# Branch C's values taken next to A's, a one-tile rotary table, lambdas first, and a last product in whole blocks and halves

## The chip, the cores and the metric

The kernel runs on one core of a Trainium2 chip. Its time is device microseconds (us) of one execution. The engines are TensorE (PE in the profile; PEld are its weight loads), VectorE (DVE), ScalarE (ACT), GpSimd (POOL) and SyncE (SP), which only issues transfers. Each works through its own queue in order and waits there for semaphores.

## What is computed

Two layers over 512 tokens of width 1024, and a last RMSNorm. Cut to what matters:

```
h = rmsnorm(x, norm_g)
aq, ak, av, az, buv, bz, cq, ck, cv, cz, gl = split_cols(h @ w_in)
A: qa, ka = partial_rope(aq), partial_rope(ak)
   ya = rmsnorm(diff_attention(qa, ka, av, lam)) * silu(az)
B: yb = u * (causal chunk product of layernorm(gelu(v))) * silu(bz)
C: yc = (three dilated windows with v = cv, merged) * silu(cz)
merged = sum over n of sigmoid(gl_n) * (y_n @ w_branch[n])
x = x + merged @ w_out
```

`partial_rope` turns the first 16 of 64 channels by sine and cosine of position times frequency. `lam` is one number a layer, from four short vectors.

## The kernel before

Everything is kept transposed: channels on the 128 partitions, the 512 tokens along the free axis. All products run in pairs of high and low parts (`xh`, `xl` for x, `whi`, `wlo` for weights): three matmuls for each product, high by high, low by high, high by low.

**Weights.** They come as tiles `raw` of 128x1024 (512 KB) over SP's queue, two tiles deep. `slot` (L151) turns each half into a slot: ACT copies the high part to `whi` (L159), and the low part `wlo` is a subtraction (L160), every fifth on GpSimd and the others on VectorE. There are six `whi` and five `wlo` buffers, so slots are made some five ahead of TensorE. Slots of the last layer's product `w_out` from block 3 on are written straight into `xh` and `xl`, and two into `mh` and `ml`, which are free by then.

**Order of the work.** `plan()` (L49) lists the dense items of a layer. First come `vb` (B's v), `val` of A, `split` and `mix` and the first pair of A. `vb` and `val` A use `proj_M` (L446): x is the stationary operand, 512 weight columns stream, and four token blocks are summed in four banks; x is the unnormalised `xuh`/`xul` there, and the norm's factor is applied when the bank is emptied. `split` makes `xh`/`xl` of the normalised x, which all later items read, and `mix` makes `mh`/`ml`. Then the two attentions run (`attention_a`, `attention_c`); between their steps `fill()` (L1029) pulls dense items, as many as `cost()` allots to the stretch. `val` of C stands at the end of A's list; it uses `proj_N` (L435) with 256 streamed columns and the normalised x. After C follow the gates and branch products, and `out`.

**The last product.** `i_out` (L789) multiplies by `w_out` in eight blocks of 128 channels. In the last layer it does so for the left 256 tokens in all eight blocks and then for the right 256, whose first block is followed by the final norm of the left half (`final(LT)`); `final(RT)` ends the kernel.

**The rotary table.** `tables()` (L301) splits position times frequency into two parts, multiplies each by five pieces of 1/(2 pi) and reduces each product to a fraction of a turn, in steps of 128x32 on GpSimd. ACT takes sine and cosine, and `trig` goes through DRAM (L352) into `cosr` and `sinr`, on the same SP queue as the weights. `lambdas()` (L358) loads `tab` and `lam_in` and computes lambda on VectorE and ACT; it is called in the first layer's `split`.

A scheduler sets each engine's order from the code, a priority for the slots and its own estimate of times.

Of the kernel before, what the change touches and what calls it, by code (L numbers as in the profile page):

```python
# [34 lines left out]
LOMOD = 5  # L35
FILLS = 25
# [12 lines left out]
def plan():  # L49

    start = [("vb",), ("val", BR_A), ("split",), ("mix",), ("pp", BR_A, 0)]
    a = [("pp", BR_A, 1), ("pp", BR_A, 2), ("u2", 0)] + [("pp", BR_A, i) for i in range(3, 6)] + [("vbn",), ("u2", 2), ("pp", BR_C, 0), ("val", BR_C)]
# [16 lines left out]
def item_units(it):  # L69
    kind = it[0]  # L70
    if kind == "vb" or it == ("val", BR_A):
        return [("M", C_VB if kind == "vb" else C_AV, k) for k in range(4)]
    if kind == "val":
        return [("N", C_CV + 256 * b, k) for b in range(2) for k in range(2)]
# [25 lines left out]
def hybrid_kernel(ctx: ExitStack, tc, xT, posr, wpack, tabs, cvec, pvec, rvec, lamv, sguw, outT):  # L100
# [62 lines left out]
    def weights():
        for l in range(DEPTH):
            for g in GROUPS:
# [67 lines left out]
    cv = const.tile([P, 8], F32, name="cv")  # L233
# [67 lines left out]
    def tables():  # L301
# [16 lines left out]
        ah = t32(F32R)
        V.tensor_copy(out=ah, in_=ang)
        al = t32()  # L320
        G.tensor_tensor(out=al, in0=ang, in1=ah.bitcast(F32), op=ALU.subtract)
        turns = t32()
        m, k = t32(), t32()
        M0, M1 = 1.5 * 2.0**23, 1.5 * 2.0**35
        parts, rest = [], 0.15915494309189533576888376337251436203445964574
        for j in range(5):
            e = math.floor(math.log2(abs(rest)))
            q = math.floor(rest * 2.0 ** (11 - e)) * 2.0 ** (e - 11)
            parts.append(q)
            rest -= q  # L330

        def frac(t, big):
            for mg in ((M1, M0) if big else (M0,)):
                G.tensor_scalar(out=k, in0=t, scalar1=mg, scalar2=mg, op0=ALU.add, op1=ALU.subtract)
                G.tensor_tensor(out=t, in0=t, in1=k, op=ALU.subtract)
# [9 lines left out]
        sn, nsn, cs = t32(), t32(), t32()  # L345
# [39 lines left out]
    ahead()  # L385

# [38 lines left out]
    def proj_T(ps, src):  # L425
        for i, (wh, wl) in enumerate(take(2)):
            wh, wl = (w.rearrange("p (k c) -> p k c", k=4) for w in (wh, wl))
            for k in range(4):
# [4 lines left out]
                yield 0.65  # L433

    def proj_N(ps, us, tb, src):  # L435
        ts = slice(tb * P, (tb + 1) * P)
        for kc in range(KC):
            wh, wl = (w.rearrange("p (k c) -> p k c", k=2)[:, kc % 2, :] for w in us[kc // 2])
            mh, ml = src(kc)
            T.matmul(ps, lhsT=mh[:, ts], rhs=wh, start=kc == 0, stop=False)  # L440
            T.matmul(ps, lhsT=ml[:, ts], rhs=wh, start=False, stop=False)  # L441
            T.matmul(ps, lhsT=mh[:, ts], rhs=wl, start=False, stop=kc == KC - 1)  # L442
            if kc % 2:
# [114 lines left out]
    def layer(l, xu, parts):  # L558
# [142 lines left out]
        def i_val(br):  # L701
            if br == BR_A:
# [86 lines left out]
        def i_out():  # L789
            xn[0] = x_ = X()  # L790
            parts = []
            for c in [LT, RT] if last else [slice(0, S)]:
                for e in range(8):
                    xr = t2k("sh", name="xr")[:, c]
                    nc.scalar.dma_start(out=xr, in_=(xT[e, :, c] if l == 0 else x1d[e, :, c]))
                    ps = ps_to()[:, c]
                    if not last:
                        yield from proj_T(ps, merged)
                    else:
                        if c is LT:  # L800
                            parts.append(take(2))
                        for i, (wh, wl) in enumerate(parts[e]):
                            wh, wl = (w.rearrange("p (k c) -> p k c", k=4) for w in (wh, wl))
                            for k in range(4):
                                kc = 4 * i + k
                                mh, ml = merged(kc)
                                mm3(ps, wh[:, k, :], wl[:, k, :], mh[:, c], ml[:, c], kc == 0, kc == KC - 1)
                                yield 0.325
                    xf = (x_.raw(e) if c.start == 0 else x_.f[e // 2][:, e % 2, :])[:, c]
                    V.scalar_tensor_tensor(out=xf, in0=ps, scalar=0.5, in1=xr, op0=ALU.mult, op1=ALU.add)  # L810
                    if last:
                        x_.square(e, c, True)
                    else:
                        x_.take(e, l + 1)
                        nc.sync.dma_start(out=x1d[e], in_=xf)
                    if c is RT and e == 0:
                        final(LT)
# [219 lines left out]
        def cost(first, after):  # L1037
            flat = {"val": 20.8, "vbn": 0.0}
# [17 lines left out]
def _tables():  # L1056
# [10 lines left out]
    cvec = np.zeros((P, 8), np.float32)  # L1067
# [5 lines left out]
def _pack(i):  # L1073
# [4 lines left out]
    for l in range(DEPTH):  # L1078
# [3 lines left out]
        for n, u in enumerate(UNITS):  # L1082
# [4 lines left out]
            elif u[0] == "N":  # L1087
                a = wi[4 * u[2] : 4 * u[2] + 4, :, u[1] : u[1] + 256].transpose(1, 0, 2)
# [50 lines left out]
```

## Time and profile before

| | us |
|---|---|
| median of 3 runs | 1151.81 (1148.14 to 1153.46) |
| profiled execution | 1150.43 |
| its span, first to last instruction | 1148.7 |
| TensorE busy | 1107.1 |
| VectorE busy | 821.6 |
| ACT busy | 601.7 |
| GpSimd busy | 515.7 |

TensorE is the busiest engine by far. Its busy time is made of instructions that overlap, so that the sum of their durations is larger than it. `L12` is line 12 of the kernel. A wait names the engine, tile and line that ended it; of several causes it names the last one seen, so that the name can be beside the point.

### The profile page before, as it was taken

To read this page: it belongs to the slowest core of one execution; us is meant where nothing else is said; L and a number is where in the kernel's file an instruction comes from. 1 tells how busy PE (TensorE), PEld (TensorE's weight loads), DVE (VectorE), ACT (ScalarE), POOL (GpSimd) and SP (SyncE) were. 2 spreads that over 40 slices of the span, in tenths; PEclk is the share of its full clock that TensorE was granted. 3 is DMA by queue.
4 is the path that set the end of the run, shared out by engine and by line. 5 is a ranking of instruction groups with operands and counts; after the bars stand their busy time and mean duration, and the time that the engine had idled before them with its cause. 6 is when DMAs were issued, how large, how long until landed. Compare 5 with 4: busy or idle time off the path is not lost.

```text
span 1148.7 us, 18512 instructions
## 1 busy us (share of the span) xinstructions
PE 1107.1 (96%) x6732; PEld 964.8 (84%) x6732; DVE 821.6 (72%) x1503; ACT 601.7 (52%) x1293; POOL 515.7 (45%) x487
## 2 busy tenths in 40 slices
PE   6989999999999999999997999999999999999977
PEld 4768889978779999998886788898787999999976
DVE  5698777567759888874568777746787887877533
ACT  5665655555855444444456464646677544544321
POOL 6664453135333766653342534322343365766312
PEclk9999999999999999999998999999999999999989
DMA  6222211221212332334523121313121133332423
GB/s 199 93 92 79 88 71 59 92 74 56 74 52 96 110 105 80 110 120 139 200 74 91 56 92 56 95 52 96 52 93 56 56 111 110 93 110 80 132 93 101
DMA packets 35643, 106.01 MB, mean 92 GB/s; under 512 B 4768, under 2 KB 8864, under 8 KB 35552
## 3 DMA queue, kind: packets, MB, share of 16 engines
q1 hardware_dynamic: 29936, 98.50, 26.7%
q10 hardware_dynamic: 5616, 6.34, 1.7%
q8 instruction: 53, 0.87, 0.3%
q14 instruction: 38, 0.31, 0.1%
HBM read 100.57 MB, written 4.24 MB: 91 GB/s over the span
## 4 chain that ended last, share of the span: by engine, by line
PE 83%; DVE 6%; POOL 3%; DMA 3%; issue 3%; ACT 2%; POOLq 0%; DVEq 0%; ACTq 0%
PE ps_pj L417 15%; PE ps_pj L419 14%; PE ps_pj L418 14%; PE ps_to L417 8%; PE ps_to L419 8%; PE ps_to L418 8%; PE ps_s L854 4%; PE ps_to L893 2%; PE ps_to L999 2%; PE ps_to L924 1%; DMA raw<-in_wpack 1%; PE ps_pj L441 1%; PE ps_pj L440 1%; PE ps_pj L442 1%; DVE wlo L160 1%
## 5 line engine op out<-in xcount | busy, mean ns | idle before, releaser
L159 ACT ACTIVATE whi<-raw 128x512 fp32r<-128x512 f32 x314 | 194.0, 627 | 240.4 <-DMA raw<-in_wpack 98.5
L160 DVE TENSOR_TENSOR wlo<-raw,whi 128x512 fp32r<-128x512 f32 x251 | 209.4, 839 | 99.8 <-PE ps_pj L419 33.3
L417 PE MATMUL ps_pj<-xh,whi 128*128 128x512 f32 (+1 forms) x544 | 210.9, 388 | 9.2 <-ACT va L707 7.0
L419 PE MATMUL ps_pj<-xh,wlo 128*128 128x512 f32 (+1 forms) x544 | 206.6, 380 | 0.0
L418 PE MATMUL ps_pj<-xl,whi 128*128 128x512 f32 (+1 forms) x544 | 204.9, 377 | 0.0
L160 POOL TENSOR_TENSOR wlo<-raw,whi 128x512 fp32r<-128x512 f32 x63 | 86.9, 1379 | 177.0 <-PE ps_pj L419 69.1
L417 PEld LDWEIGHTS ps_pj<-xh,whi 128*128 128x128 f32 x544 | 103.2, 190 | 30.6 <-ACT va L707 7.8
L419 PEld LDWEIGHTS ps_pj<-xh,wlo 128*128 128x128 f32 x544 | 103.1, 189 | 19.9 <-issue 2.1
L418 PEld LDWEIGHTS ps_pj<-xl,whi 128*128 128x128 f32 x544 | 103.4, 190 | 16.7 <-issue 0.7
L160 DVE TENSOR_TENSOR wlo<-t,whi 128x512 fp32r<-128x512 f32 x90 | 95.5, 1078 | 27.8 <-ACT whi L159 15.7
L159 ACT ACTIVATE whi<-t 128x512 fp32r<-128x512 f32 x112 | 65.6, 624 | 61.1 <-DVE t L180 37.9
L417 PE MATMUL ps_to<-mh,whi 128*128 128x256 f32 x320 | 90.5, 283 | 0.7 <-DVE zs L538 0.7
L418 PE MATMUL ps_to<-ml,whi 128*128 128x256 f32 x320 | 90.5, 283 | 0.0
L419 PE MATMUL ps_to<-mh,wlo 128*128 128x256 f32 x320 | 90.3, 283 | 0.0
L869 ACT ACTIVATE pr<-pr,nm 128x256 f32<-128x256 f32 (+3 forms) x128 | 70.7, 553 | 28.5 <-DVE nm L865 28.2
L471 POOL TENSOR_TENSOR rsh<-rsh,sinr 128x512 f32<-128x512 f32 x32 | 43.7, 1365 | 84.8 <-DVE rsh L469 79.1
L865 DVE CUSTOM_DVE_ANT_0 pr<-ps_s,tab 128x256 f32<-128x256 f32 (+3 forms) x128 | 56.7, 484 | 22.8 <-PE ps_s L854 21.7
L419 PE MATMUL ps_to<-xh,wlo 128*128 128x256 f32 x240 | 67.9, 283 | 0.0
L417 PE MATMUL ps_to<-xh,whi 128*128 128x256 f32 x240 | 67.9, 283 | 0.0
L418 PE MATMUL ps_to<-xl,whi 128*128 128x256 f32 x240 | 67.8, 283 | 0.0
L417 PEld LDWEIGHTS ps_to<-mh,whi 128*128 128x128 f32 x320 | 61.4, 192 | 1.1 <-DVE zs L538 0.9
L774 POOL TENSOR_TENSOR acc<-acc,zs 128x512 f32<-128x512 f32 x32 | 51.6, 1617 | 23.9 <-DVE zs L773 22.7
(260 smaller groups left out, 3022.6 us busy)
## 6 DMA issues: line engine op xcount, KB each, us to landing
raw<-in_wpack SPq DMA_DIRECT2D x174, 512.0 KB
xf<-in_xT SPq DMA_DIRECT2D x8, 256.0 KB
xr<-in_xT ACTq DMA_DIRECT2D x8, 256.0 KB
x1d<-xf SPq DMA_DIRECT2D x8, 256.0 KB
xr<-x1d ACTq DMA_DIRECT2D x16, 128.0 KB
raw<-in_wpack SPq DMA_DIRECT2D x4, 256.0 KB
out<-xf SPq DMA_DIRECT2D x8, 128.0 KB
out<-xf ACTq DMA_DIRECT2D x8, 128.0 KB
```

Of the source, the lines that this page charges most:

```text
L159: A.activation(out=hi, in_=src, func=AF.Copy)
L160: (G if made[0] % LOMOD == 0 else V).tensor_tensor(out=lo, in0=src, in1=hi.bitcast(F32), op=ALU.subtract)
L417: T.matmul(ps, lhsT=wh, rhs=mh, start=first, stop=False)
L418: T.matmul(ps, lhsT=wh, rhs=ml, start=False, stop=False)
L419: T.matmul(ps, lhsT=wl, rhs=mh, start=False, stop=last)
L471: G.tensor_tensor(out=sh, in0=sh, in1=sinr, op=ALU.mult)
L774: G.tensor_tensor(out=acc[d], in0=acc[d], in1=th, op=ALU.add)
L854: T.matmul(pss[m][:, at[i]], lhsT=q[HALF[m], a, qs], rhs=k[HALF[m], b, :W], start=t == 0, stop=t == 2)
L865: V.tensor_tensor_reduce(out=o, in0=pss[m][:, at[i]], in1=tab[:, 0 if br == BR_A else 1, S - W :], op0=ALU.add, op1=ALU.min, scale=-0.125, ...
L869: A.activation(out=o, in_=o, func=AF.Exp, scale=-1.0, bias=nm[:, m : m + 1], accum_out=den[:, m : m + 1],)
L893: T.transpose(pt[:, j, :], pr[:, m, j * P : (j + 1) * P], ident)
L999: T.matmul(po_[m][:, c], lhsT=v[:, j, 2 * h + m, :], rhs=pt[:, j, :], start=j + s_ == 0, stop=j == i and s_ == 1,)
```

## The change

Five edits. C's values are projected right after A's, with `proj_M`, from the unnormalised x, and the factor is applied as the banks are emptied; `proj_N` goes. The first `bz2` pair moves from C's list into A's. The rotary reduction works on one tile of 128x320 (two parts times five pieces), with the pieces in `cv`. `lambdas()` is called before the layers. The first 32 slots have no subtraction on GpSimd. In the last layer blocks 0 to 3 of the last product run over all 512 tokens, and blocks 4 to 7 in halves, with their slots in `xh`/`xl`.

```
-    start = [("vb",), ("val", BR_A), ("split",), ("mix",), ("pp", BR_A, 0)]
-    a = [...("vbn",), ("u2", 2), ("pp", BR_C, 0), ("val", BR_C)]
-    c = [("pp", BR_C, i) for i in range(1, 6)] + [("bz2", 0), ("bz2", 2)]
+    start = [("vb",), ("val", BR_A), ("val", BR_C), ("split",), ("mix",), ("pp", BR_A, 0)]
+    a = [...("vbn",), ("u2", 2), ("bz2", 0), ("pp", BR_C, 0)]
+    c = [("pp", BR_C, i) for i in range(1, 6)] + [("bz2", 2)]
...
-            (G if made[0] % LOMOD == 0 else V).tensor_tensor(out=lo, ...)
+            (G if made[0] % LOMOD == 0 and made[0] > FIRST_G else V).tensor_tensor(out=lo, ...)
...
-                    if g[0] == "O" and g[1] >= NSLOT // 2 and l == DEPTH - 1:
+                    if g[0] == "O" and g[1] >= KC // 2 and l == DEPTH - 1:
+                        k = 2 * g[1] + i - KC
+                        dst = xh[:, k, :], xl[:, k, :]
...
-        for j, q in enumerate(parts):
-            for i, a in enumerate((ah.bitcast(F32), al)):
-                dst = turns if i + j == 0 else m
-                G.tensor_scalar(out=dst, in0=a, scalar1=q, scalar2=None, op0=ALU.mult)
-                frac(dst, j == 0)
-                if i + j:
-                    G.tensor_tensor(out=turns, in0=turns, in1=m, op=ALU.add)
-        frac(turns, False)
+        G.tensor_tensor(out=t.rearrange("p (a j c) -> p a j c", a=2, j=5), in0=hl..., in1=cv[:, 2:12]..., op=ALU.mult)
+        frac(t, k, M1)
+        frac(t, k, M0)
+        V.tensor_reduce(out=turns, in_=t.rearrange("p (i c) -> p c i", i=10), axis=AX.X, op=ALU.add)
+        frac(turns, kk, M0)
...
     ahead()
+    lambdas()
...
-                    ps = ps_pj()[:, :256]
-                    yield from proj_N(ps, us, tb, xs)
-                    A.activation(out=o[:, :, 0:64], in_=p4, func=AF.Copy)
-                    V.tensor_tensor(out=o[:, :, 64:128], in0=p4, in1=o[:, :, 0:64].bitcast(F32), op=ALU.subtract)
+            banks = [ps_to() for _ in range(4)]
+            yield from proj_M(banks, xu.pair, {})
+                A.activation(out=o[:, :, 0:64], in_=p8, func=AF.Copy, scale=r)
+                V.scalar_tensor_tensor(out=o[:, :, 64:128], in0=p8, scalar=r, in1=o[:, :, 0:64].bitcast(F32), op0=ALU.mult, op1=ALU.subtract)
...
+            todo = [(e, slice(0, S)) for e in range(KC // 2 if last else KC)]
+            if last:
+                todo += [(e, c) for c in (LT, RT) for e in range(KC // 2, KC)]
+            for e, c in todo:
...
-                    if c is RT and e == 0:
+                if c is RT and e == KC // 2:
                         final(LT)
...
-            flat = {"val": 20.8, "vbn": 0.0}
+            flat = {"vbn": 0.0}
```

How the order moves at the start of the kernel, in three places. SP's queue, from the first full weight tile; `trig` and the copies behind it are the rotary table. Before:

```order
L141 DMA raw<-in_wpack 128x1024
L359 DMA tab<-in_tabs 128x1024
L141 DMA raw<-in_wpack 128x1024 x4
L352 DMA trig<-r_133 128x32 x3
L356 DMA sinr<-trig 8x512
```

The same place now:

```order
L141 DMA raw<-in_wpack 128x1024
L338 DMA tab<-in_tabs 128x1024
L340 DMA lam_in<-in_lamv 128x512
L141 DMA raw<-in_wpack 128x1024
L331 DMA trig<-r_133 128x32 x3
L335 DMA sinr<-trig 8x512 x2
```

Three weight tiles that stood ahead of `trig` now stand behind it (four half-size loads come before this place in both), and `lam_in` stands ahead.

VectorE, from the norm's `dg` to the first `wlo` after the scaling of x (`xf<-xf,pv,rbc`). Before:

```order
L408 TENSOR_TENSOR dg<-ident,rp 128x512
L160 TENSOR_TENSOR wlo<-raw,whi 128x512
L348 SCALAR_TENSOR_TENSOR r_133<-r_133 128x32
L160 TENSOR_TENSOR wlo<-raw,whi 128x512
L490 SCALAR_TENSOR_TENSOR gw<-gw,vb 128x512 x2
L160 TENSOR_TENSOR wlo<-raw,whi 128x512
L586 SCALAR_TENSOR_TENSOR xf<-xf,pv,rbc 128x512 x8
L492 SCALAR_TENSOR_TENSOR vb<-gth,vb 128x512 x2
L490 SCALAR_TENSOR_TENSOR gw<-gw,vb 128x512
L423 TENSOR_TENSOR xl<-xf,xh 128x512
L490 SCALAR_TENSOR_TENSOR gw<-gw,vb 128x512
L160 TENSOR_TENSOR wlo<-raw,whi 128x512
```

Now:

```order
L160 TENSOR_TENSOR wlo<-raw,whi 128x512 x2
L388 TENSOR_TENSOR dg<-ident,rp 128x512
L160 TENSOR_TENSOR wlo<-raw,whi 128x512 x2
L459 SCALAR_TENSOR_TENSOR gw<-gw,vb 128x512
L160 TENSOR_TENSOR wlo<-raw,whi 128x512
L459 SCALAR_TENSOR_TENSOR gw<-gw,vb 128x512
L461 SCALAR_TENSOR_TENSOR vb<-gth,vb 128x512
L555 SCALAR_TENSOR_TENSOR xf<-xf,pv,rbc 128x512 x8
L568 BN_STATS st<-vb 128x6
L461 SCALAR_TENSOR_TENSOR vb<-gth,vb 128x512
L459 SCALAR_TENSOR_TENSOR gw<-gw,vb 128x512 x2
L403 TENSOR_TENSOR xl<-xf,xh 128x512 x3
```

Two `wlo` stand ahead of `dg` now, five in all ahead of the scaling; behind these twelve rows come two `wlo` more.

GpSimd, from the end of the rotary table: `xl` is the low part of the normalised x, `tm` a step of `mix`. Before:

```order
L347 TENSOR_SCALAR r_133<-r_133 128x32
L423 TENSOR_TENSOR xl<-xf,xh 128x512
L507 TENSOR_TENSOR tm<-xf 128x512
L423 TENSOR_TENSOR xl<-xf,xh 128x512
L507 TENSOR_TENSOR tm<-xf 128x512
L160 TENSOR_TENSOR wlo<-raw,whi 128x512
```

Now:

```order
L381 TENSOR_TENSOR rp<-ro,mhalf 128x4
L403 TENSOR_TENSOR xl<-xf,xh 128x512 x2
L476 TENSOR_TENSOR tm<-xf 128x512
L403 TENSOR_TENSOR xl<-xf,xh 128x512
L476 TENSOR_TENSOR tm<-xf 128x512
L403 TENSOR_TENSOR xl<-xf,xh 128x512
```

The first `tm` has two `xl` ahead of it, and no `wlo` stands between.

## Rows read from the trace of the kernel before

**Rows 1.** The page, part 1: busy time, share of the span, instructions.
```profile
PE 1107.1 (96%) x6732; PEld 964.8 (84%) x6732; DVE 821.6 (72%) x1503; ACT 601.7 (52%) x1293; POOL 515.7 (45%) x487
```

**Rows 2.** Waits of TensorE: tile and line, releaser, us in total, times, longest.
```profile
PE ps_pj L417 <- ACT va L707: 7.0, 2, 6.3
PE ps_to L453 <- ACT whi L159: 5.6, 2, 5.2
PE ps_to L455 <- POOL wlo L160: 5.1, 1, 5.1
PE ps_pj L455 <- POOL wlo L160: 3.4, 1, 3.4
PE ps_to L417 <- ACT xh L159: 2.8, 1, 2.8
PE ps_to L417 <- DVE xf L810: 2.5, 1, 2.5
PE ps_pj L417 <- DVE neglam L374: 2.2, 1, 2.2
PE ps_pj L417 <- ACT zs L545: 1.6, 1, 1.6
```

**Rows 3.** Stretches: length, busy PE, PEld, DVE, ACT, POOL, PEclk, DMA share, GB/s.
```profile
20.00:40.00 20.00, 14.89 (x59) 11.69 (x58) 6.26 (x12) 8.30 (x15) 14.75 (x35) 0.83 0.24 83
60.00:80.00 20.00, 17.20 (x75) 13.61 (x74) 20.00 (x37) 10.36 (x19) 11.32 (x8) 1.00 0.34 106
...
620.00:640.00 20.00, 17.89 (x67) 14.57 (x68) 11.26 (x20) 10.53 (x17) 8.58 (x7) 0.83 0.29 102
1080.00:1100.00 20.00, 17.48 (x122) 16.81 (x121) 9.65 (x14) 6.68 (x12) 5.02 (x4) 0.91 0.28 95
1100.00:1120.00 20.00, 16.43 (x120) 15.81 (x120) 5.21 (x10) 3.87 (x8) 2.34 (x4) 0.91 0.30 90
```

**Rows 4.** Groups by line and shape: count, busy us, mean ns, idle before.
```profile
L160 POOL TENSOR_TENSOR wlo<-raw,whi 128x512 fp32r<-128x512 f32 x63 | 86.9, 1379 | 177.0 <-PE ps_pj L419 69.1 <-ACT whi L159 38.6 <-PE ps_to L419 24.1
...
L442 PE MATMUL ps_pj<-wlo,xh 128*128 128x256 f32 x128 | 36.3, 284 | 0.0
...
L454 PE MATMUL ps_pj<-whi,xul 128*128 128x512 f32 x32 | 12.5, 389 | 0.0
```

**Rows 5.** Timeline of TensorE, ends of two undisturbed runs: start, us.
```profile
195.08 0.28 PE L441 MATMUL ps_pj<-whi,xl 128*128 128x256 f32 x1
...
197.71 0.28 PE L442 MATMUL ps_pj<-wlo,xh 128*128 128x256 f32 x1
...
593.87 0.39 PE L453 MATMUL ps_pj<-whi,xuh 128*128 128x512 f32 x1
...
602.71 0.39 PE L453 MATMUL ps_pj<-whi,xuh 128*128 128x512 f32 x1
```

**Rows 6.** Timeline of SP's queue at the rotary table: start, us.
```profile
36.72 1.28 SPq L352 DMA_DIRECT2D trig<-r  x3
...
42.22 0.36 SPq L141 DMA_DIRECT2D raw<-in_wpack  x1
```

**Rows 7.** Timeline of VectorE and GpSimd, 41 to 65 us: start, us.
```profile
41.06 5.38 DVE L586 SCALAR_TENSOR_TENSOR xf<-xf,pv,rbc 128x512 f32<-128x512 f32 x8
...
45.99 6.41 POOL L423 TENSOR_TENSOR xl<-xf,xh 128x512 fp32r<-128x512 f32 x1 [8.56 <-ACT xh L422]
...
49.37 0.69 DVE L160 TENSOR_TENSOR wlo<-raw,whi 128x512 fp32r<-128x512 f32 x1
...
55.49 1.10 DVE L423 TENSOR_TENSOR ml<-tm,mh 128x512 fp32r<-128x512 f32 x1 [1.85 <-ACT mh L422]
...
64.42 2.34 DVE L160 TENSOR_TENSOR wlo<-raw,whi 128x512 fp32r<-128x512 f32 x2
```

**Rows 8.** Chain that ended last, at the last product: start, us, what.
```profile
1087.94 3.66 DMA raw<-in_wpack
```

**Rows 9.** Stretch of both attentions of layer 1, columns as in rows 3.
```profile
80.00:345.00 265.00, 262.82 (x1568) 220.44 (x1567) 188.74 (x426) 158.19 (x389) 102.41 (x111) 0.99 0.22 72
```

More of the change, by code (lines that the diff above doesn't have):

```diff
@@ L35 @@
 LOMOD = 5
+FIRST_G = 32
 FILLS = 25
@@ L70, in item_units @@
     kind = it[0]
[L71 to L74, printed above, removed]
+    if kind in ("vb", "val"):
+        c = C_VB if kind == "vb" else C_AV if it[1] == BR_A else C_CV
+        return [("M", c, k) for k in range(4)]
     if kind in ("u2", "bz2"):
@@ L159, in slot @@
             A.activation(out=hi, in_=src, func=AF.Copy)
-            (G if made[0] % LOMOD == 0 else V).tensor_tensor(out=lo, in0=src, in1=hi.bitcast(F32), op=ALU.subtract)
+            (G if made[0] % LOMOD == 0 and made[0] > FIRST_G else V).tensor_tensor(out=lo, in0=src, in1=hi.bitcast(F32), op=ALU.subtract)
         slots.append((hi, lo))
@@ L232, in hybrid_kernel @@
     ln = pv[:, 26:42].rearrange("p (l i g) -> p l i g", l=DEPTH, i=2)
-    cv = const.tile([P, 8], F32, name="cv")
+    cv = const.tile([P, 12], F32, name="cv")
     posi = const.tile([P, 32], I32, name="posi")
@@ L320, in tables @@
[L320 to L335, printed above, removed]
@@ L337, in tables @@
[L337 to L345 removed]
+        hl = sm.tile([P, 2, 32], F32R, tag="r32", bufs=1, name="r32r")
@@ new lines, in tables, with frac @@
+        t, k = (t2k("sh", name="turn")[:, :320] for _ in range(2))
+        ang, turns, kk, sn, nsn, cs, m = (r32[:, 32 * i : 32 * i + 32] for i in range(7))
+        M0, M1 = 1.5 * 2.0**23, 1.5 * 2.0**35
+        V.tensor_copy(out=ang, in_=posi)
+        V.tensor_scalar(out=ang, in0=ang, scalar1=cv[:, 0:1], scalar2=None, op0=ALU.mult)
+        V.tensor_copy(out=hl[:, 0, :], in_=ang)
+        V.tensor_tensor(out=hl[:, 1, :], in0=ang, in1=hl[:, 0, :].bitcast(F32), op=ALU.subtract)
+        def frac(t, k, mg):
+            G.tensor_scalar(out=k, in0=t, scalar1=mg, scalar2=mg, op0=ALU.add, op1=ALU.subtract)
+            G.tensor_tensor(out=t, in0=t, in1=k, op=ALU.subtract)
@@ L432, in proj_T @@
                     spent(1)
[L433 to L443, printed above, removed]
                 yield 0.65
@@ L605, in i_split @@
         def i_split():
-            if l == 0:
-                lambdas()
             for kc in range(KC):
@@ L710, in i_val @@
                 return
+            banks = [ps_to() for _ in range(4)]
+            yield from proj_M(banks, xu.pair, {})
             val[br] = v = att.tile([P, 4, 8, P], F32R, tag="vs", name="vs")
-            for b in range(2):
-                us = take(4)
-                for tb in range(4):
-                    ps = ps_pj()[:, :256]
-                    yield from proj_N(ps, us, tb, xs)
-                    p4 = ps.rearrange("p (h e) -> p h e", h=4)
-                    o = v[:, tb, 4 * b : 4 * b + 4, :]
-                    A.activation(out=o[:, :, 0:64], in_=p4, func=AF.Copy)
-                    V.tensor_tensor(out=o[:, :, 64:128], in0=p4, in1=o[:, :, 0:64].bitcast(F32), op=ALU.subtract)
-                spent(4)
+            for tb in range(4):
+                p8 = banks[tb].rearrange("p (h e) -> p h e", h=8)
+                r, o = norm["rst"][:, tb : tb + 1], v[:, tb]
+                A.activation(out=o[:, :, 0:64], in_=p8, func=AF.Copy, scale=r)
+                V.scalar_tensor_tensor(
+                    out=o[:, :, 64:128], in0=p8, scalar=r, in1=o[:, :, 0:64].bitcast(F32), op0=ALU.mult,
+                    op1=ALU.subtract,
+                )
         def i_pp(br, i):
@@ L790, in i_out @@
             xn[0] = x_ = X()
[L791 to L815, printed above, removed]
-                    if c is RT and e == 0:
-                        final(LT)
@@ new lines, in i_out @@
+            held = {}
+            todo = [(e, slice(0, S)) for e in range(KC // 2 if last else KC)]
+            if last:
+                todo += [(e, c) for c in (LT, RT) for e in range(KC // 2, KC)]
+            for e, c in todo:
+                xr = t2k("sh", name="xr")[:, c]
+                nc.scalar.dma_start(out=xr, in_=(xT[e, :, c] if l == 0 else x1d[e, :, c]))
+                ps = ps_to()[:, c]
+                if not last or e < KC // 2:
+                    yield from proj_T(ps, merged)
+                else:
+                    if c is LT:
+                        held[e] = take(2)
+                    for i, (wh, wl) in enumerate(held[e]):
+                        wh, wl = (w.rearrange("p (k c) -> p k c", k=4) for w in (wh, wl))
+                        for k in range(4):
+                            kc = 4 * i + k
+                            mh, ml = merged(kc)
+                            mm3(ps, wh[:, k, :], wl[:, k, :], mh[:, c], ml[:, c], kc == 0, kc == KC - 1)
+                            yield 0.325
+                xf = (x_.raw(e) if c.start == 0 else x_.f[e // 2][:, e % 2, :])[:, c]
+                V.scalar_tensor_tensor(out=xf, in0=ps, scalar=0.5, in1=xr, op0=ALU.mult, op1=ALU.add)
+                if last:
+                    x_.square(e, c, True)
+                else:
+                    x_.take(e, l + 1)
+                    nc.sync.dma_start(out=x1d[e], in_=xf)
+                if c is RT and e == KC // 2:
+                    final(LT)
@@ L1066, in _tables @@
     tabs = np.stack([causal, logc], axis=1).astype(np.float32)
-    cvec = np.zeros((P, 8), np.float32)
+    cvec = np.zeros((P, 12), np.float32)
+    rest = 0.15915494309189533576888376337251436203445964574
+    for j in range(5):
+        e = math.floor(math.log2(abs(rest)))
+        q = math.floor(rest * 2.0 ** (11 - e)) * 2.0 ** (e - 11)
+        cvec[:, 2 + j] = cvec[:, 7 + j] = q
+        rest -= q
     cvec[:, 0] = np.repeat(500000.0 ** (-np.arange(8) * 2.0 / 16.0), 16).astype(np.float32)
```

25 lines of the change are left out of this document (6 added, 19 removed).

## The prediction

> **What bounds the kernel now.** I read the page's first part, TensorE's waits, the granted clock, the distance between neighbouring matmuls, and then the other engines in the stretches where TensorE waits. TensorE is busy for 1107.1 of 1148.7 us [rows 1], so what the others do counts only where it stops TensorE: 41.6 us of idle time in all. The list of waits [rows 2] puts the large ones in three places. In the first 80 us: two waits for a `wlo` that GpSimd (POOL) makes (5.1 and 3.4), 2.2 for a bank put down to "neglam", and 0.4 and 0.6 inside the rows `whi L159` and `va L707`. (Of the 5.6 of `whi`, 5.2 is the start, before any weight is there; it stays.) At the start of layer 2: the 6.3 of `va L707`. In the last product: 2.8 and 2.5. Behind such waits the clock is at its lower level of 1.2 GHz for a while. The mean of 0.83 in the slices 20-40 and 620-640 and of 0.91 in 1080-1100 [rows 3] is (1-0.83)x20/0.5 = 6.8 and 3.6 us at half rate. Some of it lies in the idle time itself (until 26.2 and 622.1), so that about 2.3, 2.3 and 1.7 us of work are lost; the slice 1100-1120 reads 0.91 too, another 1.7.
>
> The trap of this profile is in the groups: a 256-column matmul has a mean of 284 ns, one of 512 columns 389 [rows 4], as if two halves cost 568 against 389. But they overlap. In an undisturbed run 39 steps of 512 columns take 602.71-593.87 = 8.84 us, 226.7 ns each; 22 steps of 256 columns take 197.71-195.08 = 2.63 us, 119.5 ns each [rows 5]. Two halves cost 239.0 against 226.7.
>
> **The change part by part.**
>
> *Fewer, wider matmuls.* C's values were 192 matmuls of 256 columns a layer and become 96 of 512; the last product's blocks 0 to 3 go from 192 to 96. That is 2x96+96 = 288 pairs merged, at 239.0-226.7 = 12.3 ns each: 3.5 us. The columns streamed stay the same.
> The Trainium skill, "TensorE: Matmul & The Clock Gate", section "Wait — 56ns, not 53.3ns?", gives a warm matmul as columns over 2.4 GHz plus about 2.5 ns fixed. By that a merged pair would save 2.5 ns and all of them 0.7 us; the rows show 12.3 ns here, and I go by the rows.
>
> *The last product.* Today each left half-block takes 24x0.1195 = 2.9 us of TensorE and needs a raw tile whose transfer shows up with 3.66 us in the chain [rows 8]: weights cannot keep up, hence 2.8+2.5 us of waits and twice 1.7 us of slow clock. Afterwards four whole blocks take 24x0.2267 = 5.4 us each, 21.8 in all, and the weights of blocks 4 to 7 go straight into `xh`/`xl` meanwhile: four transfers of 3.66 are 14.6 us. So the waits go: 5.3+3.4 = 8.7. Late next would be the first normalising pass, which has only four right halves (11.5 us) beside it instead of eight; its eight multiplications stand on VectorE (DVE) ahead of the last two right blocks, which are not out of TensorE much before. I cost it at nothing; if it is late it is up to 3.5 us. Bounds of this part: 4 to 9.
>
> *Start of layer 2.* The wait is for the banks of A's values, which ScalarE (ACT) empties late because it stands behind `mh` copies that wait for VectorE and GpSimd. Now 96 matmuls, 21.8 us, of C's values come in between, into other banks, so that 6.3+2.3 = 8.6 goes. The weights for them are there, as slots run five ahead. Bounds: 5 to 9.
>
> *Start of layer 1.* Lost today: 0.4+5.1+2.3+3.4+0.6+2.2 = 14.0. Six of the first 32 subtractions leave GpSimd, and forty-odd 32-wide steps there become five 320-wide and two 32-wide ones. A wide one costs between nothing and the 1.38 us of a full 512-wide subtraction [rows 4]; at the upper end that is 6.9 us, and the sine is ready by about 22 us instead of 36.7, when `trig` is issued [rows 6]. So the 5.1 with its slow clock goes (7.4), and the value product of B ends some 8 us earlier.
> What is late next. On the DMA queue `trig` now stands ahead of the fifth weight tile. Issue of `trig` to the tile behind it took 42.22-36.72 = 5.5 us [rows 6]; so it is issued at about 27.5, lands 3.66 later, and A's first weights are ready at about 32. VectorE has five `wlo` that depend on these tiles queued ahead of the scaling of x, which therefore starts at about 41, as today [rows 7], although TensorE is 7 us further on. Today the next `wlo` comes 8.3 us after that start (49.37-41.06); in the new order one `gw` and one `xl` more and one `bn` fewer stand between, so some 10 us, at 51. TensorE needs it 69 matmuls into A's values (by its order), 32+69x0.2267+0.5 = 48: a wait of 3. Then GpSimd's order has two `xl` ahead of the first `tm`; `ml`, which waits for it, comes at about 57 instead of 55.5, and the first `wlo` of C's values 8.9 us after it, as today (64.42-55.49): 66, where TensorE wants it at about 60. That is 6, with some 2 us of slow clock or small waits beside them: 11 of the 14 come back in another form, because VectorE is the bound there (20.00 of 20 us in 60-80 [rows 3]). I take a saving of 3. Bounds: -4 (VectorE later by another 7) to 14 (no new wait).
> GpSimd's `xl` at 45.99 took 6.41 us [rows 7] while VectorE ran without a gap; the mean of its subtractions is 1.38 [rows 4]. The Trainium skill, "GPSIMD Engine Reference", section "1. Specifications", says that GpSimd shares its SBUF interfaces with VectorE and that VectorE instructions with two SBUF inputs contend. The moved subtractions are of that kind, so by this rule the change lengthens what stays on GpSimd; the row agrees in kind, and by the rule the start would keep more of its loss than the 11, by the row's own 5 us excess at most.
>
> *Lambdas first* costs VectorE the same small steps earlier, in a stretch where it is busy for 6.26 of 20 us [rows 3]: nothing, unless `lam_in` lands late (a wait of up to 3.66, in the bounds above).
>
> *Thinner filling of the attentions.* A's stretch loses C's values, 192x0.1195 = 22.9 us, and gets the first `bz2` pair, 48x0.2267 = 10.9; C's loses that pair. So A is 12 and C 11 us shorter a layer, and the same softmax work has to fit. In these 265 us today VectorE is busy for 188.7 and ACT for 158.2 [rows 9], which still fits into 265-23 = 242. Waits there today: 1.6 (`zs L545`) and smaller ones, some 3 in all. I let them double: a cost of 3, between 0 and 11 (a quarter of the 46 us taken out).
>
> *Sum:* 3.5+8.7+8.6+3-3 = 20.8. The profiled execution is 1150.4 us (span 1148.7 and 1.7 around it), 1.4 under the median of 1151.8: 1150.4-20.8 = 1129.6, so **1130 us**.
>
> **Rivals.**
> - *The start recovers fully*: GpSimd is free early, and VectorE's order turns out not to bind. 11 us more: 1119. For it: the page's waits name GpSimd and not VectorE; against it, the full VectorE. 0.17.
> - *The start gets worse*, by a late `trig` or `lam_in`: 7 less, 1137. 0.06.
> - *The attentions are bound by their softmax chain* (the other side): A and C do not get shorter, and all 2x23 = 46 us come back as waits: 1150.4-20.8-3+46 = 1173. It decides as soon as over half of the 46 comes back: then the gain of 23.8 without this cost is gone. For it: single short waits already stand inside these stretches; against it: TensorE is busy for 262.8 of the 265 us [rows 9]. 0.05; a partial return that leaves the time where it is: 0.08.
> - *The groups' means are the price*: 288x(568-389) = 51.6 instead of 3.5, so 1082. The starts of neighbouring matmuls exclude it almost: 0.02.
>
> **How the numbers follow.** The forecast has 0.62, its own range from the bounds 1121 to 1138. Eight in ten, with the first two rivals and part of the return: 1117 to 1143. A measurement tells 0.5%, 5.8 us, from no change: faster 0.62+0.17+0.06+0.02 = 0.87, same 0.08, slower 0.05.
>
> **What would show it.** Right: no wait of TensorE over 1 us in the last product and at layer 2's start, clock 1.0 there; waits for a `wlo` of VectorE in 45-70 us; TensorE's busy time down by about 10 (merging and slow clock). Wrong: waits on `ps_s` or `ps_to` inside the attentions of more than 10 us in all; a last product with `xh` waits; a start without any `wlo` wait.

## The result, and the profile after

The changed kernel takes 1135.07 us (median of 4 runs, 1133.82 to 1136.46), the kernel before 1151.38 beside it: a ratio of 0.9854 (95% interval 0.9841 to 0.9867). That is 16.8 us less by the ratio and 16.3 in the medians. The forecast was 20.8 less, 1130. The profiled execution took 1134.42 with a span of 1132.7, against 1148.7 before: 16.0 in the spans.

The page's first part, as in [rows 1]:

```profile
PE 1101.8 (97%) x6444; PEld 943.7 (83%) x6444; DVE 815.2 (72%) x1500; ACT 598.4 (53%) x1281; POOL 487.8 (43%) x438
```

TensorE has 5.3 us less busy time and 30.9 us of idle time instead of 41.6. The list of its waits, as in [rows 2]:

```profile
PE ps_pj L424 <- DVE wlo L160: 7.5, 1, 7.5
PE ps_to L422 <- ACT whi L159: 5.8, 2, 5.3
PE ps_pj L398 <- DVE yB L403: 2.5, 2, 1.8
PE ps_to L424 <- DVE wlo L160: 1.9, 3, 1.2
PE ps_s L393 <- DVE dg L388: 1.5, 1, 1.5
PE ps_to L397 <- ACT whi L159: 1.3, 3, 0.7
PE ps_to L399 <- DVE wlo L160: 1.0, 2, 0.5
```

The 6.3 at layer 2's start and the 2.8 and 2.5 of the last product are gone; so are the two waits for GpSimd's `wlo`. In their place stand one wait of 7.5 for a `wlo` of VectorE, and small new ones for `yB`, `whi` and `wlo`. The stretches of [rows 3], and two more of which the text speaks:

```profile
20.00:40.00 20.00, 18.81 (x84) 14.83 (x84) 11.62 (x27) 11.85 (x21) 2.36 (x4) 1.00 0.41 119
40.00:60.00 20.00, 12.48 (x49) 9.95 (x48) 19.61 (x24) 10.24 (x19) 9.83 (x6) 0.84 0.07 26
60.00:80.00 20.00, 20.00 (x88) 16.48 (x88) 16.08 (x28) 13.07 (x23) 5.57 (x3) 0.99 0.45 132
620.00:640.00 20.00, 19.60 (x87) 15.92 (x86) 10.97 (x18) 13.53 (x23) 4.08 (x4) 1.00 0.46 145
1080.00:1100.00 20.00, 20.00 (x100) 17.00 (x99) 10.86 (x17) 8.08 (x14) 5.03 (x4) 1.00 0.45 145
1100.00:1120.00 20.00, 20.00 (x168) 19.95 (x167) 5.25 (x14) 2.50 (x6) 4.79 (x7) 1.00 0.18 53
...
360.00:380.00 20.00, 17.78 (x108) 15.39 (x107) 18.21 (x26) 8.75 (x16) 9.49 (x8) 1.00 0.30 93
```

The clock reads 1.00 where it read 0.83 and 0.91. The slow stretch has moved from 20-40 to 40-60 us, where the clock was 1.00 before.

To size each term I took the starts of all TensorE rows and subtracted from each distance the undisturbed one (226.7 ns at 512 columns, 119.5 at 256, for small tiles one fixed value in both kernels). What is left is waiting and slow clock, called the gaps below: 88.5 us before and 75.5 after.

| | forecast gain | measured gain by these gaps |
|---|---|---|
| fewer, wider matmuls | 3.5 | 3.5 (288 pairs at 12.3 ns, taken off with the distances: not measured by itself here) |
| last product | 8.7 | 10.0 (14.6 to 4.6) |
| start of layer 2, 560-660 us | 8.6 | 8.4 (11.1 to 2.7) |
| start of layer 1, 0-80 us | 3 | 3.3 (18.8 to 15.5) |
| attentions and the stretch behind them | -3 | -8.7 (41.9 to 50.6) |

They add to 16.5. From the first to the last start of a matmul the kernel is 16.4 shorter, and what lies around them is 0.4 longer: 16.0 in the spans. Another value for the small tiles moves a term by some 0.5. Four terms came out; the fifth is the miss.

### The profile page after: what moved, and what is told of

Same layout as the page of the kernel before. It is cut to its first block, busy times and chain, and to the rows that moved or that the text cites. A ratio compares the mean times of both kernels' runs of the same rounds, so it can differ in the third digit from the quotient of the medians.

```text
span 1132.7 us, 17894 instructions
## 1 busy us (share of the span) xinstructions
PE 1101.8 (97%) x6444; PEld 943.7 (83%) x6444; DVE 815.2 (72%) x1500; ACT 598.4 (53%) x1281; POOL 487.8 (43%) x438
## 4 chain that ended last, share of the span: by engine, by line
PE 86%; DVE 8%; DMA 2%; issue 2%; ACT 1%; POOL 1%; POOLq 0%; SPq 0%; DVEq 0%; ACTq 0%
PE ps_pj L397 15%; PE ps_pj L398 15%; PE ps_pj L399 15%; PE ps_to L397 8%; PE ps_to L399 8%; PE ps_to L398 8%; PE ps_s L823 4%; PE ps_to L862 2%; PE ps_to L424 2%; PE ps_to L968 2%; PE ps_to L893 2%; PE ps_to L422 2%; PE ps_to L423 2%; DVE wlo L160 2%; DVE xf L555 1%
## 5 line engine op out<-in xcount | busy, mean ns | idle before, releaser
L160 DVE TENSOR_TENSOR wlo<-raw,whi 128x512 fp32r<-128x512 f32 x261 | 212.1, 820 | 113.9 <-ACT whi L159 36.9
L397 PE MATMUL ps_pj<-xh,whi 128*128 128x512 f32 (+1 forms) x544 | 208.5, 383 | 0.8 <-ACT whi L159 0.5
L160 POOL TENSOR_TENSOR wlo<-raw,whi 128x512 fp32r<-128x512 f32 x55 | 76.8, 1397 | 139.1 <-PE ps_pj L399 53.4
L160 DVE TENSOR_TENSOR wlo<-t,whi 128x512 fp32r<-128x512 f32 x88 | 92.5, 1070 | 16.1 <-ACT whi L159 9.8
L838 ACT ACTIVATE pr<-pr,nm 128x128 f32<-128x128 f32 (+3 forms) x128 | 70.6, 553 | 32.9 <-DVE nm L834 32.7
L834 DVE CUSTOM_DVE_ANT_0 pr<-ps_s,tab 128x128 f32<-128x128 f32 (+3 forms) x128 | 57.4, 485 | 28.6 <-PE ps_s L823 26.4
L399 PEld LDWEIGHTS ps_to<-mh,wlo 128*128 128x128 f32 x320 | 61.1, 192 | 0.6 <-DVE wlo L160 0.4
```

Of the source, the lines that this page charges most:

```text
L160: (G if made[0] % LOMOD == 0 and made[0] > FIRST_G else V).tensor_tensor(out=lo, in0=src, in1=hi.bitcast(F32), op=ALU.subtract)
L397: T.matmul(ps, lhsT=wh, rhs=mh, start=first, stop=False)
L399: T.matmul(ps, lhsT=wl, rhs=mh, start=False, stop=last)
L834: V.tensor_tensor_reduce(out=o, in0=pss[m][:, at[i]], in1=tab[:, 0 if br == BR_A else 1, S - W :], op0=ALU.add, op1=ALU.min, scale=-0.125, ...
L838: A.activation(out=o, in_=o, func=AF.Exp, scale=-1.0, bias=nm[:, m : m + 1], accum_out=den[:, m : m + 1],)
```

## Experiments: the parts alone

A ratio is to the kernel before, timed beside the run. "Less" without another word means less than that kernel, by the ratio. Against the changed kernel the difference is given in the medians and in the ratios.

**The last product alone** (`i_out` and its slots as after, all else as before).

> The kernel before with the new last product alone (four whole blocks, four in halves, their weights in xh/xl). Theory (my sum, term by term): waits and slow clock of the last product go, 8.7, and 96 merged pairs give 96 x 12.3 ns = 1.2, so 9.9 less than before: a ratio of 0.9914. Rival 1, the sizes overlap and the first normalising pass is late by up to 3.5: 6.4 less, 0.9944. Rival 2, the groups' means are the price of a pair: 96 x 179 ns = 17.2 and 8.7, 25.9 less, 0.9775.

Measured: 1142.6, ratio 0.9908 (0.9895 to 0.9922), 10.6 us less. The interval is 9.0 to 12.1 us: the theory's 9.9 lies in it, and both rivals are out. In its trace TensorE has no wait in the last product and waits only 1.0 and 1.5 in the final norm behind it, so the first normalising pass is hidden.

**C's values alone.**

```
+    start = [("vb",), ("val", BR_A), ("val", BR_C), ("split",), ...]
+    a = [... ("u2", 2), ("bz2", 0), ("pp", BR_C, 0)]
+    c = [... ("bz2", 2)]
...
```

> The kernel before with C's values next to A's alone (proj_M, the first bz2 pair in A's list); rotary table, lambdas, GpSimd's subtractions and last product as before. Theory: layer 2's start gives 8.5, merging 192 pairs 2.4, and the attentions, filled more thinly, take back some 8.6 (the difference of the gaps between matmuls after and before), so that without the start of layer 1 it is 2.3 less than before: 0.998; the old table keeps the start's first stall, and C's values put their 22 us between, so the start itself is within 3 of before either way: 0.995 to 1.001. Rival, my sum as it stands (attentions cost 3): 8 less, 0.993. Rival, all stalls of the start go with it too, because C's values give the other engines 22 us to catch up: 14 more less, 0.983.

Measured: 1149.3, 0.9968 (0.9956 to 0.9981), 3.7 less. This is the theory's range; my sum (8 less) and the full recovery are out. The rest of the edit (`i_val`, the weight units, `flat`) is as in the changed kernel. The wait for `va` at layer 2's start is gone here too (0.4 is left). So this edit gives its 8.5 and takes most of it back in the attentions.

**Rotary table, lambdas and the first 32 slots alone.**

> The kernel before with the one-tile rotary table, the lambdas first and no subtraction on GpSimd among the first 32 slots; C's values and last product as before. Theory: the early stalls (5.1 and its 2.3 of slow clock) go and most of it comes back as a wait for a wlo of VectorE at 45 to 65 us, so 3 less than before, 0.997 (bounds 0.990 to 1.003). Rival, VectorE binds only because C's values ask for eight more low parts there: without them the start recovers by 10, 0.991.

Measured: 1151.1, 0.9984 (0.9975 to 0.9992), 1.8 less. C's values are not in the start here, and yet TensorE waits for one `wlo` of VectorE:

```profile
PE ps_pj L440 <- DVE wlo L161: 7.1, 1, 7.1
```

So the rival that blamed their eight low parts falls. The three parts add to 16.1, the whole change gives 16.8: they hardly touch each other.

## Experiments: the price of a split matmul, and the start

**Value products in pairs of 256 columns**, in the changed kernel:

```
-    T.matmul(banks[tb], lhsT=mh_[:, ts], rhs=wh, ...)
...
+    for c in [slice(0, S)] if any(ends) else [LT, RT]:
+        T.matmul(banks[tb][:, c], lhsT=m_[:, ts], rhs=w_[:, c], ...)
```

Here `ends` marks the first and the last matmul of a bank, which stay whole.

> The changed kernel with 88 of the 96 matmuls of each value product (B's v, A's and C's values, both layers) cut into two of 256 columns over the same stationary tile: 528 pairs more, same columns. Theory (distance of neighbouring starts, 12.3 ns a pair): 6.5 us, of which about 1.8 lie ahead of the 7.5 us wait at 49 us and are hidden: 4.7 more than the changed kernel's 1135.1, so 1139.8, 0.990 of before. Rival 1, the groups' means (179 ns a pair): up to 94 more, 1229. Rival 2, a fixed 2.5 ns a matmul: 1.3 more, 1136.4, 0.987 of before.

Measured: 1132.0, 0.9821 (0.9808 to 0.9835), faster than the changed kernel (3.0 in the medians, 3.8 in the ratios) with 528 matmuls more. None of the three theories had that. The timeline of TensorE has the pairs just as priced, 0.24 us from pair to pair against 0.2267 for one wide matmul:

```profile
600.08 0.40 PE L425 MATMUL ps_pj<-whi,xuh 128*128 128x256 f32 x2
600.32 0.40 PE L425 MATMUL ps_pj<-whi,xul 128*128 128x256 f32 x2
600.56 0.40 PE L425 MATMUL ps_pj<-wlo,xuh 128*128 128x256 f32 x2
```

What paid for them is the start: the 7.5 us wait is not there, and VectorE has another order of instructions, set by the scheduler. Two runs take these apart.

**The same in layer 2 only**, where layer 1's order stays.

> The changed kernel with the three value products of layer 2 alone cut into pairs of 256 columns: 264 pairs more in a stretch where TensorE does not wait; layer 1 stays as it was, order included. Theory (12.3 ns a pair): 3.2 more than 1135.1, 1138.3, 0.988. Rival 1 (2.5 ns a pair): 0.7 more, 1135.8, 0.986. Rival 2 (the groups' means, 179 ns): 47 more, 1182.

Measured: 1139.6, 0.9889 (0.9873 to 0.9906), 4.5 more than the changed kernel in the medians and 4.0 in the ratios (1.6 to 6.4 from both intervals), 15 ns a pair (6 to 24). The theory's 12.3 stands; 2.5 and 179 do not. In the profiled executions the spans differ by 4.8: 3.2 are the 264 pairs at 12.3 ns, and 1.6 are gaps in the first 80 us, where the edit changes nothing and TensorE, VectorE, ACT and GpSimd have the same order. The Trainium skill, "TensorE: Matmul & The Clock Gate", section "Wait — 56ns, not 53.3ns?", has 2.5 ns a matmul, for matmuls issued back to back. Here, where each matmul has its own weight load (6444 of both on the page), the measurement lies above that, and the measurement decides.

**B's v product only.**

> The changed kernel with only B's v product cut into pairs of 256 columns (176 pairs in both layers, of which the 88 of layer 1 have stalls beside them). The scheduler's order on VectorE changes with it as in the run before: dg ahead of the wlo, scaling of x ahead of gw, and wlo between the rows of it. Theory, the 7.5 us wait and its slow clock come from that order and not from VectorE's work, which is the same: 9.2 less and 1.1 to 2.2 more, 1127.0 to 1128.1, 0.978 of before. Rival, the earlier split run owed its time to the wider cut of A's and C's values (TensorE later, VectorE less late): then at most half of it returns here, 1132 or more, 0.982 and up.

Measured: 1129.7, 0.9797 (0.9782 to 0.9813), 5.4 less than the changed kernel in the medians, 6.6 in the ratios: between theory and rival, nearer the theory. The wait is gone; in 0-80 us the gaps fall from 15.5 to 7.9, and 176 pairs take 2.2 back. VectorE's timeline there, in the changed kernel:

```profile
33.51 0.68 DVE L388 TENSOR_TENSOR dg<-ident,rp 128x512 f32<-128x512 f32 x1
...
41.00 8.51 DVE L555 SCALAR_TENSOR_TENSOR xf<-xf,pv,rbc 128x512 f32<-128x512 f32 x8
...
51.11 3.41 DVE L459 SCALAR_TENSOR_TENSOR gw<-gw,vb 128x512 f32<-128x512 f32 x2
54.44 1.88 DVE L403 TENSOR_TENSOR xl<-xf,xh 128x512 fp32r<-128x512 f32 x3
56.25 1.28 DVE L160 TENSOR_TENSOR wlo<-raw,whi 128x512 fp32r<-128x512 f32 x2
```

and with B's v in pairs:

```profile
27.98 0.69 DVE L388 TENSOR_TENSOR dg<-ident,rp 128x512 f32<-128x512 f32 x1 [1.17 <-DMA sinr<-trig]
32.33 1.95 DVE L160 TENSOR_TENSOR wlo<-raw,whi 128x512 fp32r<-128x512 f32 x3 [3.66 <-ACT whi L159]
34.59 1.41 DVE L556 SCALAR_TENSOR_TENSOR xf<-xf,pv,rbc 128x512 f32<-128x512 f32 x2 [0.31 <-ACT rbc L553]
35.92 0.68 DVE L160 TENSOR_TENSOR wlo<-raw,whi 128x512 fp32r<-128x512 f32 x1
36.53 4.06 DVE L556 SCALAR_TENSOR_TENSOR xf<-xf,pv,rbc 128x512 f32<-128x512 f32 x6
40.50 0.68 DVE L403 TENSOR_TENSOR xl<-xf,xh 128x512 fp32r<-128x512 f32 x1
41.10 0.68 DVE L160 TENSOR_TENSOR wlo<-raw,whi 128x512 fp32r<-128x512 f32 x1
```

VectorE has as many instructions (1500). But `dg` stood behind two `wlo` that wait for the weight tile queued behind `trig`, and now stands ahead of them: the scaling of x starts 6.4 us earlier, and a `wlo` follows it after one row instead of seven. The eight scalings take 5.47 in all instead of 8.51, because GpSimd does not slow them here (see the last section). So the order bound, and with it what GpSimd did beside it, and not the number of instructions.

**All low parts of x on VectorE** (`XLG = ()`).

> The changed kernel with all eight low parts xl of x on VectorE, none on GpSimd; VectorE's order up to the scaling of x is the same. Theory 1 (GpSimd and VectorE hold each other up): the eight scalings take 5.4 us again instead of 8.5, and the two gw 1.3 instead of 3.4, five xl stand ahead of the wlo instead of three, so that TensorE goes on at about 53 instead of 57: 4 less than 1135.1, 1131, 0.981. Theory 2 (my prediction, VectorE's work is the bound there, GpSimd's relief is worth its length): four xl more are 2.4 us more on VectorE, 1137.5, 0.987; the scalings stay at about 8 us.

Measured: 1133.4, 0.9831 (0.9817 to 0.9846), 1.6 less than the changed kernel in the medians and in the spans, 2.6 in the ratios. Its interval overlaps that of the changed kernel, so the time alone says only "not slower". The rows say more. VectorE:

```profile
39.87 6.42 DVE L555 SCALAR_TENSOR_TENSOR xf<-xf,pv,rbc 128x512 f32<-128x512 f32 x8
...
48.20 1.28 DVE L459 SCALAR_TENSOR_TENSOR gw<-gw,vb 128x512 f32<-128x512 f32 x2
49.41 3.08 DVE L403 TENSOR_TENSOR xl<-xf,xh 128x512 fp32r<-128x512 f32 x5
52.42 0.68 DVE L160 TENSOR_TENSOR wlo<-raw,whi 128x512 fp32r<-128x512 f32 x1
```

and TensorE at the end of its wait, in the changed kernel and here:

```profile
56.98 1.22 PE L424 MATMUL ps_pj<-wlo,xuh 128*128 128x512 f32 x2 [7.52 <-DVE wlo L160]
...
53.15 1.22 PE L424 MATMUL ps_pj<-wlo,xuh 128*128 128x512 f32 x2 [4.32 <-DVE wlo L160]
```

Without the four `xl` on GpSimd beside them the scalings shrink by 2.1 and the two `gw` by 2.1, and TensorE goes on at 53.2 instead of 57.0. Theory 1 holds in its mechanism, and theory 2's rise did not come. The scalings stay at 6.42, not theory 1's 5.4: the last one takes 1.79, beside a `tm` of GpSimd that begins at 44.00. Of the 4 us less than half is left at the end; between 340 and 380 us the gaps are 1.4 larger than in the changed kernel.

## Experiments: the thinner attentions

Of the 8.7 us, layer 1 has 4.1. By the same gaps, its attentions themselves (80 to 340) read 19.5 before and 19.1 after; 340 to 380 reads 2.4 before and 6.9 after. Layer 2 reads 16.3 and 17.1 inside (660 to 880), 3.7 and 7.5 behind (880 to 960). So nearly all of the price is not inside the attentions but at C's end. The stretch 360-380 before (the changed kernel's is in the list above):

```profile
360.00:380.00 20.00, 20.00 (x127) 18.09 (x126) 17.13 (x25) 8.80 (x17) 12.36 (x10) 1.00 0.25 79
```

TensorE is busy for all of the 20 us before, and for 17.78 after, with the clock at 1.00 in both. TensorE's timeline at C's end before: the last matmul of C's budgeted filling, and the last two of C's output.

```profile
342.34 0.40 PE L419 MATMUL ps_pj<-xh,wlo 128*128 128x512 f32 x1
...
345.77 0.28 PE L999 MATMUL ps_to<-pth,vs 128*128 128x256 f32 x1
345.89 0.28 PE L999 MATMUL ps_to<-ptl,vs 128*128 128x256 f32 x1
```

The same in the changed kernel, and two of the waits behind:

```profile
334.99 0.39 PE L399 MATMUL ps_pj<-xh,wlo 128*128 128x512 f32 x1
335.22 0.28 PE L397 MATMUL ps_pj<-xh,whi 128*128 128x256 f32 x1
...
347.42 0.28 PE L968 MATMUL ps_to<-ptl,vs 128*128 128x256 f32 x1
...
352.19 0.39 PE L397 MATMUL ps_to<-xh,whi 128*128 128x256 f32 x1 [0.72 <-ACT whi L159]
...
365.22 0.50 PE L398 MATMUL ps_pj<-yB,whi 128*128 128x512 f32 x1 [1.84 <-DVE yB L403]
```

Before, the filling ends 3.6 us ahead of C's last matmul; after, 12.4. In layer 2 it is 4.0 and 9.0. The gate pair that stands behind C (256 columns) is pulled forward to fill the hole, and is missing where VectorE makes `y`, `yB` and the next weights.

**One more gate pair in C's list.**

```
-    end = gl[:1] + [("after", "C"), ("sgu",)] + gl[1:2]
+    end = gl[:2] + [("after", "C"), ("sgu",)]
```

> The changed kernel with one more gate pair (gl2 of A, 9.1 us of dense work a layer) pulled into the filling of C's attention; it stood behind sgu. Theory, the attentions' cost of some 8.6 comes from thin filling, 23 us a layer taken out for 4.3: 9.1 back give 1.7 a layer, 3.4 less, 1131.7, 0.982. Rival, the cost is VectorE's backlog at the end of C (the splits of y and yB), which dense items put ahead of it don't shorten, and the waits move on behind it: 1135, within 1.5, 0.984 to 0.987.

Measured: 1143.9, 0.9917 (0.9901 to 0.9932), 8.8 more than the changed kernel in the medians and 7.3 in the ratios. Both theories fall. Waits of TensorE between 330 and 380 us:

```profile
PE ps_to L968 <- ACT pth L402: 2.3, 1, 2.3
PE ps_to L968 <- DVE ptl L403: 1.6, 1, 1.6
```

The pair's matmuls stand nearly in one run, from 338.7 to 350.8, and C's last matmul comes at 362.6, 15.2 later than in the changed kernel. So the cover ends 11.8 us ahead of it again: what had been free to slide under C's last steps is used up, and C's own chain shows.

**The first `bz2` pair back in C's list** (A's filling 23 us shorter than before, C's as long).

```
-    a = [... ("u2", 2), ("bz2", 0), ("pp", BR_C, 0)]
-    c = [... ("bz2", 2)]
+    a = [... ("u2", 2), ("pp", BR_C, 0)]
+    c = [... ("bz2", 0), ("bz2", 2)]
```

> The changed kernel with the first bz2 pair (10.9 us of TensorE a layer) back at its old place in C's list, so that A's filling is 23 us shorter than before and C's as long as before. By the gaps between matmuls the 8.6 us of the thinner attentions lie at the end of C and in the 25 us behind it (340-380 and 880-960: 14.4 against 6.1 before), because the dense work of C's list is used up 12 us before C's last products. Theory, C's end pays: with the pair back the cover reaches to the end again, 6 to 8 less than 1135.1: 1127 to 1129, 0.978 to 0.980. Rival 1, thin filling costs wherever it is: A's stretch pays then, 1133 to 1137. Rival 2, VectorE is bound at C's end whatever lies beside: no change, 1135.

Measured: 1129.3, 0.9796 (0.9783 to 0.9810), 5.7 less than the changed kernel in the medians and 6.7 in the ratios: the theory. The filling ends 3.6 us ahead of C's last matmul again, and TensorE waits for nothing between 330 and 385 us:

```profile
337.69 0.40 PE L399 MATMUL ps_pj<-xh,wlo 128*128 128x512 f32 x1
...
341.24 0.28 PE L968 MATMUL ps_to<-ptl,vs 128*128 128x256 f32 x1
```

By the gaps, counted from event to event (A from its first scores to its last product; C from there to 14 us ahead of its last matmul; C's end from there to 40 us behind that matmul in layer 1 and 60 in layer 2):

| | before | changed | this run |
|---|---|---|---|
| layer 1: A, C, C's end | 5.0, 8.9, 1.7 | 6.0, 6.8, 6.4 | 4.9, 7.8, 1.7 |
| layer 2: A, C, C's end | 6.2, 5.6, 2.4 | 8.0, 5.9, 5.4 | 7.9, 7.1, 2.4 |

C's end reads as before in both layers. In layer 1 A gives up 23 us of filling without a price; in layer 2 A keeps 1.7 more than before and C 1.5, for a reason that no run shows. The other traces agree. The five kernels with both `bz2` pairs in C's list (before, the last product alone, the rotary table and lambdas alone, this run, both findings together) end their filling 3.5 to 4.0 us ahead of C's last matmul and read 1.7 and 2.4 at C's end. The six with the first pair in A's list and the gates as they were end it 12.4 and 9.0 ahead and read 5.8 to 8.0 and 5.4 to 5.7. Rival 2 is out, and rival 1 is left with some 3 us of layer 2.

**The last gate pair of C's list behind C.**

```
+    end = [("after", "C")] + gl[:1] + [("sgu",)] + gl[1:2]
```

> The changed kernel with the last gate pair of C's list (gl2 of B, 10.4 us) moved behind C: C's budgeted filling is thinner still, and the work that may be pulled under C's end and behind it is larger; the mirror of the run in which a gate pair came into C's list and the time rose by 8.8. Theory, what counts is the dense work left for C's end and the stretch behind it: 3 or more less than 1135.1, 1132 or below, 0.983. Rival, thin filling inside C is the price: 10.4 less of it a layer cost 2 a layer, 1139, 0.989.

Measured: 1142.4, 0.9909 (0.9895 to 0.9923), 7.3 more than the changed kernel in the medians and 6.3 in the ratios: the theory falls; the rival has the sign, and 4 where 6 to 7 came. The stretch that pays is now inside C, at 300 to 320 us (columns as above), with the clock at 0.74:

```profile
300.00:320.00 20.00, 16.19 (x82) 14.56 (x81) 15.23 (x26) 11.46 (x22) 8.24 (x9) 0.74 0.34 105
```

Counted as in the table above, C ahead of its end reads 14.6 and 9.6 in the two layers, where the changed kernel has 6.8 and 5.9, and C's end 4.2 and 4.0 instead of 6.4 and 5.4. So C needs its dense work both inside and at its end. Moving a gate pair either way across C's end costs 6 to 9 us; of the three moves tried, only the one that takes work from A helps.

**Both findings together**: `bz2` back in C's list, and B's v of layer 1 alone in pairs.

> The first bz2 pair back in C's list, and B's v of layer 1 alone cut into pairs of 256 columns (88 pairs), which turns VectorE's order at the start. Theory: the two parts do not touch each other, 7.5 from the start (9.2 of wait and slow clock, less 1.1 of pairs and a remainder as measured when both layers were cut) and what the pair in C's list gives alone (6 to 8): 1120 to 1122, 0.972 to 0.974. Rival, the gain of the start is taken back by the attentions as their weights and values come at other times: 1127 or more, 0.978.

Measured: 1121.2, 0.9725 (0.9712 to 0.9738), as the theory has it. That is 13.9 less than the changed kernel in the medians, 14.9 in the ratios, and 31.9 less in the medians than the kernel before beside it: the fastest version here. Its waits of TensorE in the first 80 us, of which 5.4 is the start:

```profile
PE ps_to L429 <- ACT whi L159: 5.9, 2, 5.4
PE ps_to L429 <- DVE wlo L160: 2.1, 2, 1.5
```

## Why the prediction was right, and where it was not

- *Fewer, wider matmuls, 3.5.* Right, as far as the time can tell. The distance of neighbouring starts was the price (0.24 against 0.2267 us in the rows, 15 ns a pair, 6 to 24, in the time), and the groups' means were the trap that they were taken for.
- *The last product, 8.7, and start of layer 2, 8.6.* Right in place and size: 10.0 and 8.4, no wait left in either, clock 1.00. The first normalising pass at nothing was right.
- *Start of layer 1, 3.* Right in size (3.3), and the steps up to the scaling came where they were put: `trig` at 22.35 (about 22), the tile behind it at 27.18 (27.5), the next high parts at 31.63 (32), the scaling at 41.00 (41).

```profile
22.35 1.39 SPq L331 DMA_DIRECT2D trig<-r  x3
...
27.18 38.04 SPq L141 DMA_DIRECT2D raw<-in_wpack  x7
```

  From there it failed in two ways that offset each other, so that the right size is luck. The `wlo` came at 56.25 and not at 51, so the wait is 7.5 and not 3: the eight scalings took 8.51 instead of [rows 7]'s 5.38, and the two `gw` behind them 3.41 instead of the 1.28 that they take without GpSimd beside them. These 5.3 are as much as the whole delay. The prediction had this contention, but put its price on GpSimd; VectorE paid it. TensorE was then late enough itself that the second wait, 6 at C's values, did not come. And "because VectorE is the bound there" is wrong as a reason: with the same instructions in another order the gaps fall by 7.6.
- *Thinner filling of the attentions, a cost of 3.* This is the step that failed: 8.7, within its bounds of 0 to 11, and nearly all of the distance between 20.8 and 16.8. "Still fits into 242" summed busy times over both attentions, and doubled the waits that stood in them. It did not ask where in C the filling ends, nor what the dense work behind C had to cover. The runs put the price at C's end: all that stood there goes when C gets its pair back, and some 3 of layer 2 stay inside A and C.
- *Lambdas first*: no wait for `neglam` is left. No experiment tried it alone.
- *What would show it.* TensorE's busy time fell by 5.3 and not by about 10; the slow clock did not go from the start, it moved to 40-60 us (0.84). The other signs came: a `wlo` wait in 45-70, none over 1 us at layer 2's start or in the last product; the 1.0 and 1.5 stand in the final norm.

## What to carry to other kernels

When dense work leaves a stretch that it covered, find the last matmul of the filling and the last of the chain in the timeline, and compare what is left between and behind them; a sum of busy times hides it. Then look inside the chain too: there thin filling showed a price of its own. Price a split by the distance of neighbouring starts, and never by the mean duration of a group. Where a scheduler sets the order by its own estimate, a run that changes one engine's length can change another's order: read the order before giving the time to the edit.

## What the runs showed of the hardware

GpSimd and VectorE hold each other up by whole instructions, and either of them can be the one that pays. In the run with B's v in pairs, VectorE's rows of 512 columns follow each other at 0.60 to 0.67 us from 36.5 to 46.0, and a single `xl` of GpSimd that begins meanwhile takes 7.89:

```profile
45.32 0.68 DVE L403 TENSOR_TENSOR xl<-xf,xh 128x512 fp32r<-128x512 f32 x1
...
39.27 7.89 POOL L403 TENSOR_TENSOR xl<-xf,xh 128x512 fp32r<-128x512 f32 x1 [11.32 <-ACT xh L402]
```

It ends at 47.16, 1.2 us behind the end of VectorE's last row. That is [rows 7]'s 6.41 again. In the changed kernel the same instruction gets in, and takes turns with VectorE:

```profile
43.52 3.07 POOL L403 TENSOR_TENSOR xl<-xf,xh 128x512 fp32r<-128x512 f32 x2 [14.92 <-ACT xh L402]
...
42.32 1.41 DVE L555 SCALAR_TENSOR_TENSOR xf<-xf,pv,rbc 128x512 f32<-128x512 f32 x2
43.65 1.78 DVE L555 SCALAR_TENSOR_TENSOR xf<-xf,pv,rbc 128x512 f32<-128x512 f32 x1
```

There each `xl` takes 1.5, and VectorE's eight scalings take 1.06 each in the mean against 0.67. But none of them takes 1.06: five take 0.74 each, and three, with a GpSimd row beside them, 1.78. Its two `gw` take 1.7 each, against 0.64 where GpSimd is idle. The Trainium skill, "SBUF — State Buffer", section "Terms", calls the port pair of these two engines an exclusive lock, held for a whole instruction, with the loser fully blocked. Both rows agree with it. VectorE had no gap in either run, so what let GpSimd in at 43.52 and kept it out at 39.27 these rows do not show.
